# Layer 1 mixer of a decoder trunk: key rotation of all row tiles in one set of operations, and projection pieces put in other places

## The chip, the cores and the metric

The kernel runs on one core of a Trainium2 chip. The metric is the time of one execution in microseconds (us). TensorE (PE in the profile) does the matrix products, VectorE (DVE), ScalarE (ACT) and GpSimd (POOL) the element-wise work, and SyncE (SP) issues the DMA transfers. Each engine works through its own list of instructions in order; semaphores make one wait for another.

## The reference

The program is a trunk of two layers for 512 rows of width 1024. Layer 0 mixes with two kinds of attention, layer 1 with a sparse attention whose keys an indexer picks; each layer ends in an MLP and a gated embedding (PLE). The change lies in the mixer of layer 1:

```python
cq, ckv, krope, kidx, widx = split_cols(h @ w_in, C_SPLITS)   # 384, 256, 32, 64, 8
cq, ckv = rms(cq, g_cq), rms(ckv, g_ckv)
q  = (cq @ w_uq).reshape(Bn, S, 16, 96)          # 64 plain + 32 rotated
k_rope = rope(krope)                              # 32, shared by the heads
qi = partial_rope((cq @ w_qi).reshape(Bn, S, 8, 64), pos)
ki = partial_rope(kidx)                           # 64, shared
score = einsum('bqh,bqhs->bqs', wi, relu(qi . ki)) # then causal mask, top 128 of each row
# 16 heads: softmax over the picked keys, values from ckv @ w_uv, keys from ckv @ w_uk
# layer end of PLE: h += sigmoid(h @ w_ple_gate) * (p @ w_ple_proj)
```

## The kernel before

Rows are held in four tiles of 128 (`NR` = 4). Every float32 product is taken as three matmuls of split operands (high by high, high by low, low by high; `mm3`, recorded at line L213). A weight is loaded as `raw`, cast to its high part `wh` on ACT (L139), and the low part `wl` is a subtraction (L143) on DVE or, where the table says "p", on POOL in two halves of 512 columns. The class `Stream` does this in the order in which weights are listed, four tiles ahead; `FILL_ENG` holds the engine of each weight of the fill described below. Its `raw` buffers are refilled by DMAs that SP issues in order, each after the last reader of the buffer.

The mixer of layer 1 runs like this:

- `proj(xc, 360, ...)` gives ckv, key parts and index weights of each row tile. `ckv_evac` takes them out; per row tile, `k_parts(r)` rotates the key parts into `kk` with eight DVE operations (L1179 to L1187).
- `proj(cqT, 512, ...)` gives the index queries of row tiles 1 to 3. `qi_evac` rotates them (`rope32`, L557 to L562); at row tile 2 it also transposes the last ckv tile (`lat`, L254) and the keys (`kib`, `krb`, L1210 and L1211).
- `weave(indexer(), queries())` is the scheduler of this part: the indexer yields how much slack it leaves, and pieces of the fill `queries()` are put in for it. The indexer transposes the index queries (`trq`, L1233), takes the scores (`sc`), adds them up over heads into `work` (L1253 on DVE for block 1, L1256 on POOL for blocks 2 and 3), and picks the 128 largest of each row in 16 rounds of MAX8 (L1260) and MATCH_REPLACE8 (L1261) on DVE for each of the three blocks. The fill is 8 pieces of the PLE projection (`ple`), 24 of `w_uq`, 8 of `w_uv`, 8 of `w_uk` (`kn`). The rotated part of `w_uq` is rotated on DVE (L557, L558) and added on POOL (L562).
- `head_pipe` then runs 16 heads in four stages A to D (query transposes, scores and softmax, transposes of the probabilities, values), each head a step apart (`ORDER_C`). A stage step yields its slack too; the fill there is the output projection.

PE's order is the order of the code. The other engines' instructions are ordered by a scheduler of the framework, each list fixed in advance.

Of the kernel before, what the change touches and what calls it, by code (L numbers as in the profile page):

```python
# [18 lines left out]
P = 128  # L19
# [18 lines left out]
A_SLACK = 2.6  # L38
B_SLACK, B_END = 1.1, 0.7
C_END = 0.7  # L40
IDX_SLACK = (0.2, 0.8, 1.0)
ORDER_B = (("A", 3), ("B", 1), ("C", -1), ("D", -2))
ORDER_C = (("A", 3), ("B", 2), ("C", 0), ("D", -1))
# [2 lines left out]
WARM = 10  # L46


FILL_ENG = "vppvvvvpppppp"
Z_ENG = "v" * KF  # L50
SUMS = 6
G_ENG = "vvvvvvvv"
# [6 lines left out]
def trunk_kernel(ctx, tc, A, out):  # L59
# [15 lines left out]
    def bank(tag, name):  # L75
        return psum.tile([P, 512], F32, tag=tag, name=name)
# [13 lines left out]
    def f32(ap):  # L90
        return ap.bitcast(F32)
# [88 lines left out]
    for i in range(2):  # L180
        if i == 1:
            for j in range(4):
                ws.add(A["w_cq"][j], 768)
            for j in range(4):
                ws.add(A["w_ckv"][j], 720)
            ws.add(A["w_qi"][0], 1024)
            ws.add(A["w_qi2"], 512)
            fe = FILL_ENG
            add_ple(1, fe[0:3])
            for j, c in enumerate(UQ_ORDER):  # L190
                ws.add(A["w_uq"][c], 1024, fe[3 + 2 * j])
                ws.add(A["w_uq2"][c], 512, fe[4 + 2 * j])
            for c in range(2):
                ws.add(A["w_uv"][c], 1024, fe[9 + c])
            for c in range(2):
                ws.add(A["w_uk"][c], 1024, fe[11 + c])
        for j in range(8):
            ws.add(A["w_oc" if i else "w_oab"][j], 1024)
        for j in range(KF):
            ws.add(A[f"w_mi{i}"][j], 1024, Z_ENG[j])  # L200
        wo, lo, hi = A[f"w_mo{i}"], slice(0, 512), slice(512, 1024)
        for j in range(KF // 2):
            ws.add(tsum[i, j, 0], 1024)
# [236 lines left out]
    def head_pipe(small, n, order, on, stA, kk, bias, scale, vHL, oHL, ptile, ptT, slack=0.0, end=0.0, done=None, scored=None, paired=False):  # L440


        q, p, tr, o = {}, {}, {}, [None]
# [65 lines left out]
        for i in range(-3, n + 4):  # L509
            for what, d in order:  # L510
                if 0 <= i + d < n:
                    stages[what](i + d)
            yield slack if i + order[1][1] < n else end

    def ple_proj(i, stage):

# [600 lines left out]
    with ExitStack() as ctx2:  # L1117
# [8 lines left out]
        with tc.tile_pool(name="idx", bufs=1) as ip:  # L1126
# [25 lines left out]
            def latent_t(t, r, n, xt):  # L1152
                transpose_rows(xt, lambda k: t[:, k * P : (k + 1) * P], r, list(range(n // P)))
# [16 lines left out]
            kxr = kxk[:, NR * 2 * P : NR * 2 * P + NR * 96].rearrange("p (r d) -> p r d", r=NR)  # L1170
            pool.memset(kk[:, :, 1, :], 0.0)

            def k_parts(r):
                x = kxr[:, r, :].rearrange("p (h d) -> p h d", d=32)[:, 0:2, :]
                rot = ip.tile([P, 2, 32], F32, tag="rot", bufs=2, name="rot")
                m2 = ip.tile([P, 2, 32], F32, tag="m2k", bufs=2, name="m2k")
                cs = cs32[:, r, :]
                cosb = cs[:, 0:16].unsqueeze(1).to_broadcast([P, 4, 16])
                vec.tensor_tensor(rot.rearrange("p h (t d) -> p (h t) d", d=16), x.rearrange("p h (t d) -> p (h t) d", d=16), cosb, op=ALU.mult)  # L1179
                for t in range(2):  # L1180
                    sn = cs[:, (1 + t) * 16 : (2 + t) * 16].unsqueeze(1).to_broadcast([P, 2, 16])
                    vec.tensor_tensor(m2[:, :, t * 16 : (t + 1) * 16], x[:, :, (1 - t) * 16 : (2 - t) * 16], sn, op=ALU.mult)
                vec.tensor_tensor(kk[:, r, 1, 32:64], rot[:, 0, :], m2[:, 0, :], op=ALU.add)
                vec.tensor_tensor(kk[:, r, 0, 0:32], rot[:, 1, :], m2[:, 1, :], op=ALU.add)
                vec.tensor_copy(kk[:, r, 0, 32:64], kxr[:, r, 64:96])
                vec.tensor_copy(kk[:, r, 0, 64:128], kk[:, r, 0, 0:64])
                vec.tensor_copy(kk[:, r, 1, 64:96], kk[:, r, 1, 32:64])  # L1187

            def ckv_evac(r, ps):
                if r == 0:  # L1190
                    latent_t(lat[3], 3, 384, cqT)
                else:
                    latent_t(lat["kv"], r - 1, 256, ckvT)
                act.activation(kxr[:, r, :], ps[:, 256:352], AF.Copy, scale=rstd1[:, r : r + 1])
                vec.tensor_scalar(widx[:, r, :], ps[:, 352:360], rstd1[:, r : r + 1], WI_SCALE, op0=ALU.mult, op1=ALU.mult)
                lat["kv"] = latent(ps, r, 256, 1, gckv)
                k_parts(r)

            drain(proj(xc, 360, [2] * 4, range(NR), ckv_evac))

# [2 lines left out]
            qi = slot(6, "qi").rearrange("p (r d) -> p r d", d=512)  # L1203

            def qi_evac(r, ps):
                if r == 2:
                    latent_t(lat["kv"], 3, 256, ckvT)
                    kib, krb = bank("B", "kib"), bank("B", "krb")
                    for t in range(NR):
                        pe.transpose(kib[:, t * P : (t + 1) * P], kk[:, t, 0, :], ident)  # L1210
                        pe.transpose(krb[:, t * P : (t + 1) * P], kk[:, t, 1, :], ident)  # L1211
                    for h, l, b in ((kiH, kiL, kib), (krH, krL, krb)):
                        act.copy(h, b)
                        vec.tensor_tensor(l, b, f32(h), op=ALU.subtract)
                qv = qi[:, r - 1, :].rearrange("p (h d) -> p h d", d=64)
                pv = ps.rearrange("p (h d) -> p h d", d=64)
                rope32(ip, pv[:, :, 0:32], 8, cs32[:, r, :], qv[:, :, 0:32], vec)
                act.copy(qv[:, :, 32:64], pv[:, :, 32:64])


            drain(proj(cqT, 512, [2, 1], range(1, NR), qi_evac))

            work = slot(7, "work")
            knT = [slot(12 + q, f"kn{q}").rearrange("p (a s) -> p a s", s=S) for q in range(2)]
# [39 lines left out]
            def queries():  # L1264
# [16 lines left out]
                for c in range(2):  # L1281
                    u = ws.next()
                    for q in range(4):
                        ps = bank("A", "kn")
                        for k in range(2):
                            w = slice(k * 512 + q * P, k * 512 + (q + 1) * P)
                            mm3(ps, u[0][:, w], u[1][:, w], ckvT.h(k), ckvT.l(k), k == 0, k == 1)
                        yield 1.3
                        act.copy(knT[c][:, q, :], ps)
                    ws.free()  # L1290

            weave(indexer(), queries())
# [37 lines left out]
        def pt_c(h):  # L1330
            if h % 2:
# [98 lines left out]
```

## Time and profile before

| what | before |
|---|---|
| median of three runs | 1318.71 us (1317.81 to 1320.31) |
| profiled execution | 1319.21 us, span 1317.4 us |
| PE busy | 1290.8 us, 98% of the span |
| DVE busy | 959.6 us, 73% |
| ACT busy | 655.5 us, 50% |
| POOL busy | 152.2 us, 12% |

A busy PE is not yet PE at its peak; the table says how full each engine is over the whole span, not what each stage waits for. The part of the change is the stretch from about 680 to 810 us of the span.

### The profile page before, as it was taken

To read this page: it belongs to the slowest core of one execution; us is meant where nothing else is said; L and a number is where in the kernel's file an instruction comes from. 1 tells how busy PE (TensorE), PEld (TensorE's weight loads), DVE (VectorE), ACT (ScalarE), POOL (GpSimd) and SP (SyncE) were. 2 spreads that over 40 slices of the span, in tenths; PEclk is the share of its full clock that TensorE was granted. 3 is DMA by queue.
4 is the path that set the end of the run, shared out by engine and by line. 5 is a ranking of instruction groups with operands and counts; after the bars stand their busy time and mean duration, and the time that the engine had idled before them with its cause. 6 is when DMAs were issued, how large, how long until landed. Compare 5 with 4: busy or idle time off the path is not lost.

```text
span 1317.4 us, 18700 instructions
## 1 busy us (share of the span) xinstructions
PE 1290.8 (98%) x6617; PEld 1085.0 (82%) x6617; DVE 959.6 (73%) x1765; ACT 655.5 (50%) x1229; POOL 152.2 (12%) x153
## 2 busy tenths in 40 slices
PE   9999989999999999999998999999999999999998
PEld 6887878888888888887897679998988888888877
DVE  6678767377555899868568998974765667988684
ACT  4244577243223455565455777863532234556642
POOL 4202101010000000000012753310100000000000
PEclk9999989999999999999999999999999999999999
DMA  8312231459888675664243331002689897556631
GB/s 294 111 64 73 64 121 57 160 183 299 301 282 306 235 263 193 195 197 133 81 154 104 112 112 49 2 33 97 240 297 308 303 307 247 195 194 192 193 111 48
DMA packets 91535, 227.73 MB, mean 173 GB/s; under 512 B 10289, under 2 KB 11441, under 8 KB 91441
## 3 DMA queue, kind: packets, MB, share of 16 engines
q1 hardware_dynamic: 91440, 226.54, 51.5%
q8 instruction: 52, 0.85, 0.3%
q14 instruction: 43, 0.34, 0.1%
HBM read 184.55 MB, written 41.94 MB: 172 GB/s over the span
## 4 chain that ended last, share of the span: by engine, by line
PE 87%; DVE 8%; ACT 2%; issue 2%; POOL 1%; DMA 1%; SPq 0%; DVEq 0%; ACTq 0%; POOLq 0%
PE z L213 26%; PE y L213 23%; PE pj L213 23%; PE sc L213 4%; PE pv L213 3%; DVE work L1261 2%; PE trp L378 2%; DVE m L1260 2%; PE tr L254 1%; DVE wl L143 1%; PE ak L213 1%; PE ple L213 1%; PE trq L398 1%; PE pva L213 1%; DMA xraw<-in_xT_dram 1%
## 5 line engine op out<-in xcount | busy, mean ns | idle before, releaser
L143 DVE TENSOR_TENSOR wl<-raw,wh 128x1024 fp32r<-128x1024 f32 (+3 forms) x246 | 297.6, 1217 | 67.0 <-ACT wh L139 64.4
L139 ACT CAST wh<-raw 128x1024 fp32r<-128x1024 f32 (+3 forms) x254 | 261.6, 1034 | 142.0 <-PE pj L213 45.5
L897 DVE TENSOR_TENSOR b<-b 128x512 f32<-128x512 f32 x128 | 87.9, 690 | 115.9 <-DMA b<-in_w_mo_dram 107.4
L213 PE MATMUL y<-wh,ah 128*128 128x512 f32 x432 | 168.3, 390 | 0.0
L213 PE MATMUL y<-wh,al 128*128 128x512 f32 x432 | 168.1, 389 | 0.0
L213 PE MATMUL y<-wl,ah 128*128 128x512 f32 x432 | 168.1, 389 | 0.0
L213 PE MATMUL pj<-wh,big 128*128 128x512 f32 (+1 forms) x444 | 152.5, 394 | 0.0
L221 POOL TENSOR_TENSOR st<-st,mhalf 128x1 f32<-128x1 f32 (+1 forms) x41 | 30.2, 738 | 858.4 <-DVE st L325 748.6
L213 PE MATMUL z<-hz1H,wh 128*128 128x512 f32 (+1 forms) x288 | 105.6, 367 | 0.2 <-ACT hz1H L260 0.2
L213 PE MATMUL z<-hz0H,wh 128*128 128x512 f32 (+1 forms) x288 | 105.6, 367 | 0.2 <-ACT hz0H L260 0.2
L213 PE MATMUL z<-hz0L,wh 128*128 128x512 f32 (+1 forms) x288 | 105.4, 366 | 0.3 <-DVE hz0L L261 0.3
L213 PE MATMUL z<-hz1L,wh 128*128 128x512 f32 (+1 forms) x288 | 105.4, 366 | 0.3 <-DVE hz1L L261 0.3
L213 PE MATMUL z<-hz0H,wl 128*128 128x512 f32 (+1 forms) x288 | 105.5, 366 | 0.0
L213 PE MATMUL z<-hz1H,wl 128*128 128x512 f32 (+1 forms) x288 | 105.3, 366 | 0.0
L213 PEld LDWEIGHTS pj<-wh,big 128*128 128x128 f32 x444 | 84.5, 192 | 18.7 <-issue 0.7
L213 PEld LDWEIGHTS y<-wh,ah 128*128 128x128 f32 x432 | 81.1, 188 | 16.8
L213 PEld LDWEIGHTS y<-wh,al 128*128 128x128 f32 x432 | 81.1, 188 | 16.7
L213 PEld LDWEIGHTS y<-wl,ah 128*128 128x128 f32 x432 | 81.1, 188 | 16.7
L864 ACT ACTIVATE a<-t 128x512 f32<-128x512 f32 x40 | 25.3, 632 | 117.8 <-DVE t L863 117.8
L213 PEld LDWEIGHTS z<-hz0L,wh 128*128 128x128 f32 x288 | 54.3, 189 | 9.3 <-DVE hz0L L261 0.5
L213 PEld LDWEIGHTS z<-hz1L,wh 128*128 128x128 f32 x288 | 54.3, 189 | 9.3 <-DVE hz1L L261 0.5
L213 PEld LDWEIGHTS z<-hz1H,wh 128*128 128x128 f32 x288 | 54.3, 189 | 9.3 <-ACT hz1H L260 0.5
(625 smaller groups left out, 2761.0 us busy)
## 6 DMA issues: line engine op xcount, KB each, us to landing
raw<-in_w_mi_dram SPq DMA_DIRECT2D x64, 512.0 KB, 5.2
b<-in_w_mo_dram SPq DMA_DIRECT2D x128, 256.0 KB, 5.1
tsum_dram<-b SPq DMA_DIRECT2D x128, 256.0 KB, 3.5
raw<-tsum_dram SPq DMA_DIRECT2D x32, 512.0 KB, 3.2
raw<-tsum_dram SPq DMA_DIRECT2D x64, 256.0 KB, 3.0
raw<-in_w_mo_dram SPq DMA_DIRECT2D x32, 512.0 KB, 3.7
raw<-in_w_ab_dram SPq DMA_DIRECT2D x20, 512.0 KB, 4.8
raw<-in_w_mo_dram SPq DMA_DIRECT2D x32, 256.0 KB, 2.6
```

The lines of the kernel that those rows point to most:

```text
L139: act.copy(h[:, :n], raw[:, :n])
L143: (pool if e == "p" else vec).tensor_tensor(l[:, c], raw[:, c], f32(h[:, c]), op=ALU.subtract)
L213: pe.matmul(ps, a, b, start=first, stop=last, skip_group_check=True)
L221: pool.tensor_tensor(dst, src, mhalf[:, :n], op=ALU.pow)
L254: pe.transpose(ps[:, i * P : (i + 1) * P], src(k), ident)
L378: pe.transpose(ps[:, i * P : (i + 1) * P], pt[:, OFF[qt] + kt * P : OFF[qt] + (kt + 1) * P], ident)
L398: pe.transpose(ps[:, r * P : (r + 1) * P], rows(r), ident)
L864: act.activation(at[-1][:, fb % 4, :], t, AF.Square)
L897: vec.tensor_tensor(d, x, y, op=ALU.subtract)
L1260: vec.max(m8, w)
L1261: vec.match_replace(w, m8, w, MARK)
```

## The change

The key parts of all four row tiles are rotated together after the last of them, by eight operations instead of thirty-two (`k_parts()`). The transposes of ckv and keys leave `qi_evac` and come as `keys_t()` after the last index query projection and one piece of the fill; two more pieces of the fill stand between them and the query transposes. The indexer is woven with 41 more pieces, and the last four (half of `w_uk`) go into the first steps of the heads, as `RAMP_C` lists them. The low parts of four `w_uq` tiles and of the first four output projection tiles go from DVE to POOL.

```diff
+RAMP_C = (0.0, 1.3, 2.6, 1.3)
-FILL_ENG = "vppvvvvpppppp"
+FILL_ENG = "vpppppppppppp"
...
-            ws.add(A["w_oc" if i else "w_oab"][j], 1024)
+            ws.add(A["w_oc" if i else "w_oab"][j], 1024, "p" if i and j < 4 else "v")
...
-            yield slack if i + order[1][1] < n else end
+            yield ramp[i + 3] if 0 <= i + 3 < len(ramp) else slack if i + order[1][1] < n else end
...
-            def k_parts(r):
-                x = kxr[:, r, :].rearrange("p (h d) -> p h d", d=32)[:, 0:2, :]
...
+            def k_parts():
+                rot, m2 = (ip.tile([P, 2 * NR, 2, 32], F32, tag=nm, bufs=2, name="k" + nm)[:, :NR] for nm in ("r1", "r2"))
+                x = kxr[:, :, 0:64].rearrange("p r (g d) -> p r g d", d=16)
...
-                k_parts(r)
+                if r == NR - 1:
+                    k_parts()
...
             def qi_evac(r, ps):
-                if r == 2:
-                    latent_t(lat["kv"], 3, 256, ckvT)
-                    kib, krb = bank("B", "kib"), bank("B", "krb")
...
-            drain(proj(cqT, 512, [2, 1], range(1, NR), qi_evac))
+            def keys_t():
+                latent_t(lat["kv"], 3, 256, ckvT)
+                kib, krb = bank("B", "kib"), bank("B", "krb")
...
+                        if q == 3:
+                            ws.free()
+                        act.copy(knT[c][:, q, :], ps)
                         yield 1.3
-                        act.copy(knT[c][:, q, :], ps)
-                    ws.free()
...
-            weave(indexer(), queries())
+            qg = queries()
+            drain(proj(cqT, 512, [2, 1], range(1, NR), qi_evac))
+            next(qg)
+            keys_t()
+            for _ in range(2):
+                next(qg)
+            weave(indexer(), itertools.islice(qg, 5 + 24 + 8 + 4))
...
-                        scored=lambda h: k_load(h // 2 + 1) if h % 2 and h < 15 else None), itertools.islice(og, 3))
+                        scored=lambda h: k_load(h // 2 + 1) if h % 2 and h < 15 else None, ramp=RAMP_C), itertools.chain(qg, itertools.islice(og, 3)))
```

How the lists move is shown at three places. The first is PE around the key transposes (`tr` the last ckv tile, `kib` and `krb` the keys, `pj` the index query projection, `ple` a fill piece). Before:

```order
L213 MATMUL pj<-wh,cqL_6089 128x512
L254 MATMUL tr<-ident,lat 128x128 x2
L1210 MATMUL kib<-ident,kxk 128x128
L1211 MATMUL krb<-ident,kxk 128x128
L1210 MATMUL kib<-ident,kxk 128x128
L1211 MATMUL krb<-ident,kxk 128x128
L1210 MATMUL kib<-ident,kxk 128x128
L1211 MATMUL krb<-ident,kxk 128x128
L1210 MATMUL kib<-ident,kxk 128x128
L1211 MATMUL krb<-ident,kxk 128x128
L213 MATMUL pj<-wh,cqH_6088 128x512
```

Of the change, the same place:

```order
L214 MATMUL ple<-wh,wl 128x512
L255 MATMUL tr<-ident,lat 128x128 x2
L1217 MATMUL kib<-ident,kxk 128x128
L1218 MATMUL krb<-ident,kxk 128x128
L1217 MATMUL kib<-ident,kxk 128x128
L1218 MATMUL krb<-ident,kxk 128x128
L1217 MATMUL kib<-ident,kxk 128x128
L1218 MATMUL krb<-ident,kxk 128x128
L1217 MATMUL kib<-ident,kxk 128x128
L1218 MATMUL krb<-ident,kxk 128x128
L214 MATMUL ple<-wh 128x512
```

The last nine matmuls of the projection now stand ahead of the transposes, with a `ple` piece between, and `ple` pieces follow.

The second is POOL while the index scores of blocks 2 (128x384) and 3 (128x512) are added up (`work`); `wl` are halves of low parts, `big` the added rotations. Before:

```order
L143 TENSOR_TENSOR wl<-raw,wh 128x512 x2
L1256 TENSOR_TENSOR work<-rl,mA 128x384
L1256 TENSOR_TENSOR work<-rl,work 128x384 x7
L1256 TENSOR_TENSOR work<-rl,mA 128x512
L1256 TENSOR_TENSOR work<-rl,work 128x512 x6
L562 TENSOR_TENSOR big<-r_6897,r_6898 128x8x64
L143 TENSOR_TENSOR wl<-raw,wh 128x512 x3
L1256 TENSOR_TENSOR work<-rl,work 128x512
```

Of the change:

```order
L144 TENSOR_TENSOR wl<-raw,wh 128x512 x5
L1256 TENSOR_TENSOR work<-rl,mA 128x384
L1256 TENSOR_TENSOR work<-rl,work 128x384 x2
L144 TENSOR_TENSOR wl<-raw,wh 128x512 x3
L1256 TENSOR_TENSOR work<-rl,work 128x384 x4
L563 TENSOR_TENSOR big<-r_6803,r_6804 128x8x64
L1256 TENSOR_TENSOR work<-rl,work 128x384
L1256 TENSOR_TENSOR work<-rl,mA 128x512
L1256 TENSOR_TENSOR work<-rl,work 128x512 x2
L144 TENSOR_TENSOR wl<-raw,wh 128x512 x3
L1256 TENSOR_TENSOR work<-rl,work 128x512 x2
```

Three halves more stand ahead of block 2; three halves and one rotation stand between its eight additions.

The third is PE after the scores of the first head (`sc` of `qc0`), with the query transposes `trq` of head 2. Before:

```order
L213 MATMUL sc<-kc,qc0H 128x512 x2
L213 MATMUL sc<-kc,qc0L 128x512
L398 MATMUL trq<-ident,big 128x128 x4
L213 MATMUL sc<-kc,qc1H 128x128 x2
L213 MATMUL sc<-kc,qc1L 128x128
```

Of the change:

```order
L214 MATMUL sc<-kc,qc0H 128x512 x2
L214 MATMUL sc<-kc,qc0L 128x512
L214 MATMUL kn<-ckvT,wh 128x512 x2
L214 MATMUL kn<-ckvT,wl 128x512
L214 MATMUL kn<-ckvT,wh 128x512 x2
L214 MATMUL kn<-ckvT,wl 128x512
L399 MATMUL trq<-ident,big 128x128 x4
L214 MATMUL sc<-kc,qc1H 128x128 x2
```

One `kn` piece of six matmuls stands here; two more follow the scores of head 1, and one the first probabilities' transposes.

## Rows read from the trace of the kernel before

**Rows 1.** The page: busy time of the engines, and the chain that ended last.

```profile
PE 1290.8 (98%) x6617; PEld 1085.0 (82%) x6617; DVE 959.6 (73%) x1765; ACT 655.5 (50%) x1229; POOL 152.2 (12%) x153
...
PE 87%; DVE 8%; ACT 2%; issue 2%; POOL 1%; DMA 1%; SPq 0%; DVEq 0%; ACTq 0%; POOLq 0%
```

**Rows 2.** Waits of PE from 690 to 800: engine, tile, releaser, total us, times, longest.

```profile
PE trq L1233 <- DVE qi L562: 2.0, 1, 2.0
PE tr L254 <- DVE lat L1149: 1.9, 1, 1.9
PE sc L213 <- ACT qc0H L400: 1.5, 1, 1.5
PE sc L213 <- DVE qc0L L401: 1.1, 1, 1.1
```

**Rows 3.** Stretches: length, busy us of PE, PEld, DVE, ACT, POOL, granted clock, DMA share.

```profile
705.20:708.60 3.40, 3.40 (x14) 3.11 (x15) 2.41 (x9) 2.06 (x5) 0.00 (x0) 0.52 0.23 90
...
710.30:712.40 2.10, 0.10 (x2) 0.05 (x2) 2.06 (x6) 1.52 (x3) 1.72 (x2) 1.00 0.00 0
712.40:775.00 62.60, 61.16 (x283) 45.27 (x284) 60.05 (x159) 46.59 (x93) 41.01 (x34) 1.00 0.38 118
...
790.80:794.10 3.30, 3.30 (x11) 2.90 (x12) 1.71 (x7) 1.51 (x5) 0.00 (x0) 0.50 0.57 164
```

**Rows 4.** Chain that ended last, from 719 to 797: start us, us, what.

```profile
719.94 1.08 PE sc L213 x9
...
772.93 1.87 DVE wl L143
...
788.89 1.22 DVE wl L143
...
790.76 3.46 PE sc L213 x10
...
794.66 1.91 PE sc L213 x12
```

**Rows 5.** DVE in order of time: block 1 summed, and a round that stands alone.

```profile
717.44 0.48 DVE L1253 SCALAR_TENSOR_TENSOR work<-rl,widx,mA 128x256 f32<-128x256 f32 x1 [0.84 <-ACT rl L1250]
...
732.41 0.43 DVE L1260 MAX8 m<-work 128x8 f32<-128x256 f32 x1
732.87 0.09 DVE L1261 MATCH_VALUE_LOAD work<-m,work 128x8 f32 x1
732.95 0.41 DVE L1261 MATCH_REPLACE8 work<-m,work 128x256 f32<-128x256 f32 x1
733.39 0.43 DVE L1260 MAX8 m<-work 128x8 f32<-128x256 f32 x1
```

**Rows 6.** DVE groups from 716.5 to 790.2: count, busy us, mean ns, idle before.

```profile
L143 DVE TENSOR_TENSOR wl<-raw,wh 128x1024 fp32r<-128x1024 f32 (+1 forms) x7 | 8.9, 1270 | 0.0
```

**Rows 7.** POOL groups from 706 to 790, as above.

```profile
L143 POOL TENSOR_TENSOR wl<-raw,wh 128x512 fp32r<-128x512 f32 x13 | 16.8, 1322 | 11.5 <-ACT wh L139 11.5
...
L562 POOL TENSOR_TENSOR big<-r,r 128x512 f32<-128x512 f32 x4 | 5.2, 1302 | 0.2 <-DVE r L558 0.2
```

**Rows 8.** POOL in order of time: block 2, first and last additions.

```profile
722.29 1.01 POOL L1256 TENSOR_TENSOR work<-rl,mA 128x384 f32<-128x384 f32 x1 [8.92 <-ACT rl L1255]
...
731.61 2.11 POOL L1256 TENSOR_TENSOR work<-rl,work 128x384 f32<-128x384 f32 x2 [0.69 <-ACT rl L1255]
```

**Rows 9.** DVE in order of time: one key rotation without and with POOL at work.

```profile
691.19 0.21 DVE L1179 TENSOR_TENSOR rot<-kxk,cs 128x64 f32<-128x64 f32 x1
...
700.96 0.85 DVE L1179 TENSOR_TENSOR rot<-kxk,cs 128x64 f32<-128x64 f32 x1
```

**Rows 10.** PE in order of time: the first `kn` piece, and what follows the eighth.

```profile
775.85 0.62 PE L213 MATMUL kn<-ckvT,wh 128*128 128x512 f32 x2
...
786.74 1.03 PE L398 MATMUL trq<-ident,big 128*128 128x128 f32 x8
```

**Rows 11.** DMA issues from 700 to 745: count, KB, us to landing.

```profile
ple_dram<-pl SPq DMA_DIRECT2D x8, 256.0 KB, 2.1
```

More of the change, by code (lines that the diff above doesn't have):

```diff
@@ L438, in pt_pair, with head_pipe @@
                 mp.tile([P, 1280], F32R, tag="ptl", bufs=1, name=name + "L"))
-    def head_pipe(small, n, order, on, stA, kk, bias, scale, vHL, oHL, ptile, ptT, slack=0.0, end=0.0, done=None, scored=None, paired=False):
+    def head_pipe(small, n, order, on, stA, kk, bias, scale, vHL, oHL, ptile, ptT, slack=0.0, end=0.0, done=None, scored=None, paired=False, ramp=()):
         q, p, tr, o = {}, {}, {}, [None]
@@ L1171, in trunk_kernel @@
             pool.memset(kk[:, :, 1, :], 0.0)
-            def k_parts(r):
-                x = kxr[:, r, :].rearrange("p (h d) -> p h d", d=32)[:, 0:2, :]
[L1175 to L1179, printed above, removed]
-                for t in range(2):
[L1181 to L1187, printed above, removed]
@@ new lines, in k_parts @@
+            def k_parts():
+                rot, m2 = (ip.tile([P, 2 * NR, 2, 32], F32, tag=nm, bufs=2, name="k" + nm)[:, :NR] for nm in ("r1", "r2"))
+                x = kxr[:, :, 0:64].rearrange("p r (g d) -> p r g d", d=16)
+                xt = kxr[:, :, 0:64].rearrange("p r (h t d) -> p r h t d", t=2, d=16)
+                mt = m2.rearrange("p r h (t d) -> p r h t d", d=16)
+                cosb = cs32[:, :, 0:16].unsqueeze(2).to_broadcast([P, NR, 4, 16])
+                vec.tensor_tensor(rot.rearrange("p r h (t d) -> p r (h t) d", d=16), x, cosb, op=ALU.mult)
+                for t in range(2):
+                    sn = cs32[:, :, (1 + t) * 16 : (2 + t) * 16].unsqueeze(2).to_broadcast([P, NR, 2, 16])
+                    vec.tensor_tensor(mt[:, :, :, t, :], xt[:, :, :, 1 - t, :], sn, op=ALU.mult)
+                for h, (t, c) in enumerate(((1, 32), (0, 0))):
+                    vec.tensor_tensor(kk[:, :, t, c : c + 32], rot[:, :, h, :], m2[:, :, h, :], op=ALU.add)
+                vec.tensor_copy(kk[:, :, 0, 32:64], kxr[:, :, 64:96])
+                vec.tensor_copy(kk[:, :, 0, 64:128], kk[:, :, 0, 0:64])
+                vec.tensor_copy(kk[:, :, 1, 64:96], kk[:, :, 1, 32:64])
@@ L1205, in qi_evac @@
             def qi_evac(r, ps):
-                if r == 2:
-                    latent_t(lat["kv"], 3, 256, ckvT)
-                    kib, krb = bank("B", "kib"), bank("B", "krb")
[L1209 to L1214, printed above, removed]
                 qv = qi[:, r - 1, :].rearrange("p (h d) -> p h d", d=64)
@@ L1218, in qi_evac @@
                 act.copy(qv[:, :, 32:64], pv[:, :, 32:64])
-            drain(proj(cqT, 512, [2, 1], range(1, NR), qi_evac))
+            def keys_t():
+                latent_t(lat["kv"], 3, 256, ckvT)
+                kib, krb = bank("B", "kib"), bank("B", "krb")
+                for t in range(NR):
+                    pe.transpose(kib[:, t * P : (t + 1) * P], kk[:, t, 0, :], ident)
+                    pe.transpose(krb[:, t * P : (t + 1) * P], kk[:, t, 1, :], ident)
+                for h, l, b in ((kiH, kiL, kib), (krH, krL, krb)):
+                    act.copy(h, b)
+                    vec.tensor_tensor(l, b, f32(h), op=ALU.subtract)
             work = slot(7, "work")
```

## The prediction

> **What bounds the kernel now.** I read the page first: PE is busy for 98% of the span, and 87% of the chain that ended last is PE's, 8% DVE's [rows 1]. So two things can shorten the run: time in which PE stands idle or runs at the lower clock, and the stretch where the chain is DVE's. Then the waits of PE in the mixer of layer 1: 2.0 us for the last rotated index query, 1.9 us for the last ckv tile, 1.5 and 1.1 us for the first head's query [rows 2], 6.5 us in all. Then the stretches: after the waits for ckv and for the first head the granted clock is 0.52 and 0.50 for 3.4 and 3.3 us, that is 1.2 instead of 2.4 GHz, so some 1.65 us of PE's work are lost each time; after the wait of 2.0 us it stays at 1.00 [rows 3].
>
> The last view decides: the chain. Up to 721 it is PE's (index scores); from there to 790.8 it is DVE's top-128 rounds and what stands between them, and only then PE's again [rows 4]. Between 712.4 and 775 DVE is busy for 60.05 of 62.60 us [rows 3]. So PE's own waits in this stretch are not what a gain must be read from. Two clocks run: when DVE can begin with block 1 (717.44 [rows 5]) and how much besides the rounds is on its list.
>
> **The change, part by part.** The sum is made along that chain, to the first low-part product of head 0 (790.76 [rows 4]), and then along PE.
>
> A. *The lead-in.* The keys' eight operations run once instead of four times, and the last nine matmuls of the index query projection come ahead of the transposes; three `ple` pieces more (1.4 us each: six matmuls at the spacing of a `kn` piece, (786.74 - 775.85)/8 = 1.36 us [rows 10]) are put between. PE has then no reason to stand for ckv or for the query: 1.9 + 2.0 us and 1.65 us of lost clock go, 5.5 us, of which the three earlier pieces use 4.2; the pauses between kinds of matmul, which I can't split, may give some tenths more. PE would reach the first index score 1.4 to 2.0 us earlier. But what is late next is ACT. It copies each `ple` piece into one of two buffers, and a buffer is free when its store has landed, 2.1 us after issue [rows 11]. SP issues these stores in order, and between them stand loads of `raw` buffers whose last reader is now POOL: two halves of 1.32 us per tile [rows 7], where DVE took about the time of one. The third and fourth copy therefore wait, and the casts of the index queries stand behind them on ACT. I take 0.9 us of gain for the start of block 1, with 0 and 2.0 us as ends.
>
> B. *Low parts off DVE.* Seven of the eight moved subtractions stand in the stretch of the chain, 8.9 us [rows 6]; the eighth stood before it. A round alone repeats every 0.98 us for 0.43 + 0.09 + 0.41 us of work [rows 5], so a subtraction hid little in its gaps, about 0.1 us each. Gain 8.0 us (7.5 to 8.9). POOL gets them: fourteen halves, 18.5 us at 1.32 us.
>
> C. *What POOL then delays.* POOL adds up block 2's scores, eight additions from 722.29 to 733.72 [rows 8], and DVE comes to this block at about 734, when the last lone round of block 1 is done [rows 5]: just in time. Now three halves and one rotation stand between the additions: 3 x 1.32 + 1.30 = 5.3 us [rows 7]. POOL's idle time there was about 3.0 us (the stretch of 11.4 us less eight times 1.05), and it begins 0.9 to 2.0 us earlier (A), say 1.4. It would end at about 735, and DVE, which is earlier by A and by one subtraction, would come at about 733.3. MAX8 of block 2 stands next on DVE's list, and the rest of block 1's rounds behind it. I take a wait of 2.0 us for block 2 and nothing for block 3, whose three halves stood before its last addition already; ends 0 and 5.3 (all of the added POOL work shows).
>
> The batch of keys itself runs beside POOL: one rotation took 0.21 us alone and 0.85 us while POOL worked [rows 9]; three such operations are dearer by 0.64 each, but PE needs the keys only after a `ple` piece, so it costs nothing; without that cover 1.9 us. The Trainium skill has a rule for it, in "SBUF — State Buffer", section "Who interferes with whom": DVE and GpSimd share one port pair, an operation of DVE that reads two SBUF operands and one of GpSimd that reads SBUF exclude each other for a whole instruction, and one with a single SBUF input is not touched. Rows 9 fit it. By that rule the top-128 rounds stay as fast beside a fuller POOL, but the casts of the first head's keys near the end, which can take the pair, could each be held for one of POOL's halves, so C would be 4.6 instead of 2.0 us.
>
> D. *The four `kn` pieces.* 4 x 1.36 = 5.4 us of PE [rows 10] leave the stretch where the chain is DVE's, where PE had room, and come behind the first head's scores, where the chain is PE's: +5.4 us. They would only be free if PE stood idle among the first heads, and after 790.8 it doesn't. One thing can pay back: if the wait ahead of head 0 gets short enough for the clock to stay, 1.65 us (scores of head 0 3.46 us at the lower clock, of head 1 1.91 us [rows 4]). I take half, -0.8 (0 to -1.65).
>
> E. *PE itself.* With four pieces gone PE is ahead of DVE by some 5 us, but the four projection banks are held longer: the rotations of `w_uq`'s second row tile stand behind the wait of C on DVE's list. PE may be the later one at head 0; +0.8 us (0 to 2.5).
>
> Sum: -0.9 - 8.0 + 2.0 + 5.4 - 0.8 + 0.8 = -1.5 us. The profiled execution took 1319.21 us; the median of the runs is 0.5 us lower, so the sum goes from 1318.71 to **1317.2 us**. The bounds added up linearly are -9 and +7, which no likely case reaches.
>
> A measurement of this kernel tells a change from none at about 0.2%, here 2.6 us: faster is under 1316.1, slower over 1321.4.
>
> **Rivals.**
> 1. *POOL keeps up.* C is 0, the stores don't hold ACT (A 2.0), the clock stays (1.65): -2.0 - 8.0 + 5.4 - 1.65 + 0.8 = -5.4, with half of it uncertain some -4.5: 1314.2 us. For it: POOL is idle for a good part of the stretch (41.01 busy of 62.60 us [rows 3]). Against: its additions come at a pace that ACT sets, and the new halves stand among them, not behind.
> 2. *PE's time alone counts.* All four waits (6.5 us) and both stretches of low clock (3.3 us) go and no new wait comes: -9.8, 1308.9 us. For it: PE is the busiest engine. Against: the chain runs through DVE for 70 us.
> 3. *POOL becomes the bound (slower).* One mechanism: POOL's list is in order, and each half put ahead of an addition delays the top-128 behind it. It decides from the point where block 2's last addition ends after about 738. Then C is 5.3, E 2.5, D is not paid back, and A brings nothing: -8.0 + 5.3 + 5.4 + 2.5 = +5.2: 1323.9 us. For it: POOL was done with block 2 only 0.5 us before DVE needed it.
> 4. *The waits only move.* The time saved ahead of the heads and the 5.4 us behind it are equal: 1318.7 us; this is the forecast with a slightly longer wait.
>
> **How the numbers follow.** The forecast (with rival 4, from which it can't be told by a measurement) has 0.48, and its own range is 1316.1 to 1320.5. Rival 1 has 0.32, rival 2 0.05, rival 3 0.15. Faster then is rivals 1 and 2, with 0.01 of the forecast's low edge: 0.38; within 0.2%: 0.47; slower: 0.15. For 8 in 10 the range reaches down to 1312.5 (rival 1 with its margin, without rival 2) and up to 1321.5 (without most of rival 3).
>
> **What would show it.** Right, if in the new profile: PE no longer waits at the last ckv tile and the index queries, and the granted clock stays at 1.00 there (A); no subtraction `wl` stands among the rounds, which end 5 to 7 us earlier against the start of block 1 or of the span (B); DVE waits 1 to 3 us for POOL's addition ahead of block 2 (C); the four `kn` pieces stand after head 0's scores, and PE is busy throughout (D). It is wrong if DVE doesn't wait for POOL at all (then rival 1), if the last of block 2's additions comes after 738 (rival 3), if PE shows new waits over 2 us among the first heads, or if block 1 begins no earlier than before.

## The result and the profile after

| | before | after |
|---|---|---|
| median of the runs | 1318.26 us (1315.68 to 1320.31, 4 runs) | 1331.47 us (1331.22 to 1334.64, 4 runs) |
| ratio to before, 95% interval | | 1.0104 (1.0089 to 1.0118) |
| profiled execution, span | 1319.21 us, 1317.4 us | 1331.24 us, 1329.5 us |

The change makes the kernel slower by 1.0%, some 13 us; predicted were 1317.2 us and at most 1321.5. One execution of 4539 us (of the run with the engines alone, below) is left out of all ratios. The page after, PE's, DVE's and POOL's busy time and the chain that ended last:

```profile
PE 1296.2 (98%) x6617; PEld 1088.5 (82%) x6617; DVE 951.3 (72%) x1733; ACT 656.6 (49%) x1229; POOL 168.3 (13%) x167
...
PE 88%; DVE 6%; ACT 2%; issue 2%; POOL 1%; DMA 1%; SPq 0%; DVEq 0%; ACTq 0%; POOLq 0%
```

Beside [rows 1] this hardly differs, and DVE is even busy for 8 us less: shares don't show the loss. The waits of PE do. The five longest from 690 to 830 us of the span (what waits, for whom: us in total, times, longest), beside [rows 2]:

```profile
PE sc L214 <- DVE r L559: 4.8, 1, 4.8
PE sc L214 <- ACT qc0H L401: 2.5, 1, 2.5
PE sc L214 <- ACT pl L531: 2.0, 1, 2.0
PE pj L214 <- ACT rl L1250: 1.6, 2, 0.9
PE rs L494 <- DVE qc4L L402: 1.4, 1, 1.4
```

The waits for `lat` and `qi` are gone. New are 4.8 us for a rotation and 2.0 us for the copy of a `ple` piece. In both PE waits for a PSUM bank: the index scores (`sc`) and the fill pieces take the same four banks in turn (the banks of tag "A" in the kernel), and a bank can be written again only when its last contents have been read, by ACT's copy or by DVE's rotation. Each wait has a stretch of low clock behind it (stretch: length, PE busy, PEld, DVE, ACT and POOL busy, the granted clock, DMA share and GB/s):

```profile
705.20:708.60 3.40, 3.40 (x22) 2.92 (x21) 3.37 (x13) 3.01 (x6) 1.61 (x2) 1.00 0.06 23
...
718.00:722.00 4.00, 4.00 (x17) 3.39 (x18) 2.73 (x6) 2.42 (x7) 0.00 (x0) 0.50 0.47 176
...
747.00:752.30 5.30, 0.52 (x3) 0.11 (x2) 5.30 (x17) 0.00 (x0) 3.90 (x5) 0.95 0.57 198
752.30:762.00 9.70, 8.94 (x18) 5.12 (x18) 6.99 (x21) 3.17 (x6) 5.02 (x4) 0.50 0.00 0
```

The first row is the stretch that had 0.52 in [rows 3]: it is at 1.00 now. The last one is the dear one: after 4.8 us without work PE runs 9.7 us at 0.50, 1.2 instead of 2.4 GHz, so with 8.9 us busy it does 4.5 us of full-clock work. By this estimate the wait and its clock cost 9 us of PE's time together. In the same way the wait of 2.0 us, which ends at 717.8, has six us at 0.50 behind it (718 to 724).

DVE's list in order of time, around what it waits for (start, us, line and operation; the idle time before it in brackets):

```profile
718.75 0.48 DVE L1253 SCALAR_TENSOR_TENSOR work<-rl,widx,mA 128x256 f32<-128x256 f32 x1 [1.76 <-ACT rl L1250]
...
724.38 1.07 DVE L1253 SCALAR_TENSOR_TENSOR work<-rl,widx,work 128x256 f32<-128x256 f32 x2 [2.20 <-ACT rl L1250]
725.49 0.43 DVE L1260 MAX8 m<-work 128x8 f32<-128x256 f32 x1
...
740.69 0.56 DVE L1260 MAX8 m<-work 128x8 f32<-128x384 f32 x1 [2.30 <-POOL work L1256]
...
748.90 0.83 DVE L1262 TENSOR_SCALAR biast<-work 128x256 f32<-128x256 f32 x1
...
750.12 0.40 DVE L559 TENSOR_TENSOR r<-pj,cs 128x256 f32<-128x256 f32 x1
...
751.76 0.40 DVE L559 TENSOR_TENSOR r<-pj,cs 128x256 f32<-128x256 f32 x1
...
765.13 1.16 DVE L1260 MAX8 m<-work 128x8 f32<-128x512 f32 x2 [5.84 <-POOL work L1256]
...
794.40 1.49 DVE L1262 TENSOR_SCALAR biast<-work 128x512 f32<-128x512 f32 x1
```

The same places in the kernel before: block 1's first round, block 3's first round and its mask.

```profile
722.08 0.43 DVE L1260 MAX8 m<-work 128x8 f32<-128x256 f32 x1
...
753.74 1.14 DVE L1260 MAX8 m<-work 128x8 f32<-128x512 f32 x2
...
788.54 0.43 DVE L1262 TENSOR_SCALAR biast<-work 128x512 f32<-128x512 f32 x1
```

The additions of block 1 begin at 718.75 (before 717.44 [rows 5]), and its first round at 725.49, 3.4 us later than before: the last two additions wait another 2.2 us, in the stretch of half clock. Block 2 waits 2.3 us for POOL, the rotations that PE's banks wait for stand behind block 1's last round (its mask is at 748.90), and block 3 begins at 765.13, where before it began at 753.74. From there to the mask of block 3 it is 29.3 us; before it was 34.8. So some 11 us are lost ahead of block 3 and 5.5 regained in it. The chain that ended last, beside [rows 4], goes through these places (start us, us, what):

```profile
748.08 0.92 DVE work L1261 x2
...
752.31 1.62 PE sc L214 x3
...
760.76 1.48 PE sc L214 x3
...
763.82 1.29 POOL work L1256
765.13 1.14 DVE m L1260 x2
```

From block 1's last rounds it goes to PE's late scores at half clock, over POOL's last addition to block 3. PE's list at head 0 and behind it:

```profile
796.55 0.47 PE L214 MATMUL sc<-kc,qc0L 128*128 128x128 f32 x1 [1.02 <-DVE qc0L L402]
...
799.67 0.63 PE L214 MATMUL kn<-ckvT,wh 128*128 128x512 f32 x2
...
803.40 0.62 PE L214 MATMUL kn<-ckvT,wh 128*128 128x512 f32 x2
...
809.51 0.71 PE L214 MATMUL kn<-ckvT,wh 128*128 128x512 f32 x2
```

Head 0's first low-part product comes at 796.55 instead of 790.76 [rows 4], +5.8 us; the `kn` pieces add 5.5 us (1.38, 2.75 and 1.39 at these three places) and the new wait at `rs` 1.4. That is +12.7 us, 0.6 more than the span grew (+12.1).

### The profile page after: what moved, and what is told of

Its sections match the earlier page's. It is cut to its first block, busy times and chain, and to the rows that moved or that the text cites. A ratio compares the mean times of both kernels' runs of the same rounds, so it can differ in the third digit from the quotient of the medians.

```text
span 1329.5 us, 18684 instructions
## 1 busy us (share of the span) xinstructions
PE 1296.2 (98%) x6617; PEld 1088.5 (82%) x6617; DVE 951.3 (72%) x1733; ACT 656.6 (49%) x1229; POOL 168.3 (13%) x167
## 4 chain that ended last, share of the span: by engine, by line
PE 88%; DVE 6%; ACT 2%; issue 2%; POOL 1%; DMA 1%; SPq 0%; DVEq 0%; ACTq 0%; POOLq 0%
PE z L214 26%; PE pj L214 23%; PE y L214 23%; PE sc L214 4%; PE pv L214 3%; PE trp L379 2%; PE ak L214 2%; DVE work L1261 1%; PE tr L255 1%; DVE m L1260 1%; PE ple L214 1%; PE trq L399 1%; POOL wl L144 1%; DVE wl L144 1%; PE pva L214 1%
## 5 line engine op out<-in xcount | busy, mean ns | idle before, releaser
L144 DVE TENSOR_TENSOR wl<-raw,wh 128x1024 fp32r<-128x1024 f32 (+3 forms) x238 | 286.7, 1211 | 68.9 <-ACT wh L140 65.9
L214 PEld LDWEIGHTS z<-hz0H,wh 128*128 128x128 f32 x288 | 54.3, 189 | 9.1 <-ACT hz0H L261 0.5
```

The costliest lines, as they stand in the source:

```text
L144: (pool if e == "p" else vec).tensor_tensor(l[:, c], raw[:, c], f32(h[:, c]), op=ALU.subtract)
L214: pe.matmul(ps, a, b, start=first, stop=last, skip_group_check=True)
```

## The experiments

Ratios are to the kernel before, run on the same chip beside it, with their 95% interval; 0.1% is 1.3 us. The median of the kernel before differs by up to 1.2 us from one set of runs to the next (1318.1 to 1319.3), so kernels are compared by their ratios.

**Which part loses: parts undone.** First four parts were undone or relieved in the changed kernel.

The low parts of `w_uq` back on DVE:

```diff
-FILL_ENG = "vpppppppppppp"
+FILL_ENG = "vppvvvvpppppp"
```

> The four low parts of the w_uq tiles go back from POOL to DVE; the four of the output projection stay on POOL, all else as in the changed kernel (1331.5 us). Theory 'POOL's list' (the halves among the additions of blocks 2 and 3 make DVE late, and through DVE's rotations the projection banks and PE): the wait of 2.3 us at block 2 and most of PE's 4.8 us behind the rotations go, with the low clock behind it (some 4.8 us); three subtractions of 1.27 us come back among DVE's rounds: 1331.5 - 2.3 - 4.8 - 4.8 + 3.8 = about 1323.5 us, and block 3 begins some 8 us earlier. Rival 'stores' (PE is late because ACT's copy of a ple piece waits for a store behind raw loads): SP still waits, only for DVE instead of POOL, so at most 2 us come back and 3.8 go: 1331 to 1335 us. Rival 'four kn pieces behind the scores': not touched, so 1335 us.

1332.67 us, 1.0110 (1.0097 to 1.0123). The moved halves of `w_uq` among the additions are not the cause: without them PE waits even longer for a rotation (7.6 us instead of 4.8), and DVE still waits for POOL (5.9 us instead of 8.1).

```profile
PE sc L214 <- DVE r L559: 7.6, 1, 7.6
...
DVE m L1260 <- POOL work L1256: 5.9, 2, 4.5
```

In the changed kernel and here, POOL itself waits for ACT, and so for the scores, ahead of block 3's last addition (3.7 us and 1.9 us): here POOL is late for block 3 because the scores come late, and the theory of POOL's list falls for it.

The `kn` pieces ahead of the heads again:

```diff
-            weave(indexer(), itertools.islice(qg, 5 + 24 + 8 + 4))
+            weave(indexer(), qg)
...
-... ramp=RAMP_C), itertools.chain(qg, itertools.islice(og, 3)))
+... ), itertools.islice(og, 3))
```

> The four kn pieces stand ahead of the heads again (no fill in the ramp), all else as in the changed kernel (1331.5 us). Theory 'kn costs what it adds' (step D as predicted: PE had room ahead of head 0): 1331.5 - 5.4 = 1326 us. Rival 'PE has no room left': PE lost some 7 us in waits and as much at the lower clock before block 3, so that ahead of head 0 it waits only 2.5 + 1.0 us for the first query; the pieces then fill these 3.5 us and push the rest on: 1331.5 - 3.5 = 1328 us. Rival 'no part in it': 1331.5 us, if PE is the late one at head 0 anyway.

1329.09 us, 1.0082 (1.0061 to 1.0103): 0.2% back, nearer to "PE has no room left". But this interval overlaps that of the changed kernel, so the gain isn't shown.

Four stages for the `ple` pieces (a stage is the buffer that a piece is copied into and stored from):

```diff
-                yield from ple_proj(1, lambda q: ip.tile([P, 512], F32, tag="pl", bufs=2, name="pl"))
+                pls = slot(13, "pls").rearrange("p (a s) -> p a s", s=S)
+                yield from ple_proj(1, lambda q: pls[:, q % 4, :])
...
```

The lines left out take the slots of `kn` only when their halves begin; so do all later runs that use one of these slots.

> ple pieces are copied into four buffers instead of two (in a slot that is idle until the last kn pieces), all else as in the changed kernel (1331.5 us). Theory 'stores': ACT no longer waits for a store (2.96 and 0.95 us), PE reaches the index scores without its wait of 2.0 us and without the 6 us at the lower clock: the scores start 3 us earlier, and if the time from there on is set by PE and ACT it comes through whole: 1328.5 us. Rival 'POOL's list': block 2's additions get their scores earlier, but the halves of the low parts stand at the same places and wait for the same loads; DVE still waits for block 2 and PE for the rotations: 1331 us, less 1 at the most.

1326.75 us, 1.0064 (1.0050 to 1.0079): 0.40% back, 5 us, where 3 were expected. What was taken away is this, in the changed kernel (the lists of SP, ACT and PE in order of time; an SP row of several issues covers the waiting between them):

```profile
698.73 11.39 SPq L156 DMA_DIRECT2D raw<-in_w_uq_dram  x4
710.17 0.42 SPq L532 DMA_DIRECT2D ple_dram<-pl  x1
...
713.60 0.60 ACT L531 ACTIVATE pl<-ple 128x512 f32<-128x512 f32 x1 [2.96 <-DMA ple_dram<-pl]
...
717.83 0.79 PE L214 MATMUL sc<-kiT,qiH 64*128 64x256 f32 x2 [1.99 <-ACT pl L531]
```

The first store stands behind four loads of `raw`, which SP can only issue as buffers come free; ACT's third copy waits for it, and behind this copy stand the casts of the index queries. With four stages DVE begins block 3 at 762.47 instead of 765.13, still after 5.83 us of waiting, and PE still waits 4.8 us for the rotation: a loss of its own.

The rotated rows copied out of their banks by ACT:

```diff
+                qt_c = slot(13, "qtc").rearrange("p (a s) -> p a s", s=S)
...
+                            t = qt_c[:, r, :]
+                            act.copy(t, ps)
-                            rope32(ip, ps.rearrange(...), ...)
+                            rope32(ip, t.rearrange(...), ...)
...
```

> ACT copies each rotated w_uq row out of its projection bank first, and DVE rotates the copy, so that the bank is free without DVE; all else as in the changed kernel (1331.5 us). Theory 'bank held': PE's wait of 4.8 us for a rotation goes and with it the lower clock up to 762 (another 4.8 us lost), block 3's scores and its last addition come up to 9 us earlier: four copies of some 0.6 us on ACT come on top: 1323 to 1325 us. Rival 'POOL's list alone': DVE comes to block 3 when POOL has its additions done, and POOL has the same halves to do: the wait of PE goes but block 3 begins no more than 2 us earlier: 1329.5 to 1331.5 us. Rival 'kn': not touched, 1331.5 us.

1333.39 us, 1.0120 (1.0104 to 1.0135). PE's wait for rotations and DVE's waits for POOL are both gone, as the theory of the held bank has it, but the time isn't back. By operation from 715 to 800 us (count, busy, mean ns of one):

```profile
L558 DVE TENSOR_TENSOR r<-qtc,cs 128x256 f32<-128x256 f32 x8 | 7.0, 875 | 2.7 <-ACT qtc L1276 2.7
...
L559 DVE TENSOR_TENSOR r<-qtc,cs 128x256 f32<-128x256 f32 x8 | 6.3, 786 | 0.0
```

The rotations, now with two operands in SBUF, take 875 and 786 ns instead of 415 and 405 in the changed kernel: 6.7 us more on DVE's list, and PE waits 10.6 us for head 0. The edit takes the wait away and brings a price of its own, so by itself it settles nothing.

**The parts alone, and the order of the fill.** Then the rotated `w_uq` tile was put second, with nothing made dearer:

```diff
-UQ_ORDER = (2, 0, 1)
+UQ_ORDER = (0, 2, 1)
```

> The changed kernel (1331.5 us) with w_uq's column tiles in the order plain, rotated, plain (before: rotated first): the eight pieces that need DVE's rotations come eight pieces later on PE, when few scores are left. Theory 'bank held' (PE stands 4.8 us behind rotations that wait on DVE's list behind block 1's rounds and POOL's block 2, and then runs at the lower clock): the wait and the clock's 4.8 us go, block 3's scores and their last addition come 8 to 10 us earlier, no instruction becomes dearer: 1322 us; PE may then wait for rotations later, which holds only fill. Rival 'POOL's list': the halves of low parts among the additions stay, DVE still waits some 2 us for block 2 and 5 us for block 3: 1329 to 1331 us.

1326.16 us, 1.0068 (1.0048 to 1.0088): 0.36% back. PE's wait for the rotation is gone and block 3 begins at 756.32; but five of the eight row tiles are rotated only from 774 to 783, PE waits 4.1 us for ACT's copies of plain pieces, and the 1322 us expected were not reached.

The pieces ahead alone (the kernel before, with `k_parts()`, `keys_t()` and the three `next(qg)`; engines and `kn` as before):

> The kernel before (1318.5 us) with the first part alone: keys rotated in one set, three ple pieces ahead; low parts on DVE as before, kn ahead of the heads. Theory 'bank held' (the pieces ahead bring the rotated w_uq rows three pieces earlier among the scores, where DVE is not yet free): a new wait of PE of 4 to 7 us for a rotation with low clock behind it, less the waits and clock saved in the lead-in (5.5 us) and plus ACT's wait for stores: about 1322 us. Rival 'POOL's list' (the halves on POOL cause the loss): none of them here, so the lead-in's gain shows: 1314 to 1317 us.

1328.13 us, 1.0078 (1.0061 to 1.0094). So three quarters of the loss are in this part, more than expected. Its waits of PE and ACT:

```profile
PE sc L214 <- DVE r L559: 7.6, 1, 7.6
PE sc L214 <- ACT pl L531: 1.7, 1, 1.7
...
ACT pl L531 <- DMA ple_dram<-pl: 3.6, 2, 2.9
```

Both new waits are there without any of the moved low parts. The batch of keys was not run apart from the pieces.

The engines alone (the kernel before, with `FILL_ENG` and the `w_oc` entry of the change):

> The kernel before (1318.5 us) with the low parts of four w_uq and four output projection tiles on POOL, and nothing else. Step B as predicted with C of 2: 1318.5 - 8 + 2 = 1312.5 us. Theory 'PE has little room' : the rounds end 6 us earlier, but PE waits only 1.5 + 1.1 us for head 0 and loses 1.65 us of clock there, so it gains no more than that: 1314 to 1315 us. Rival 'POOL's list' (the halves among the additions make DVE and PE late): 1322 us or more.

The median is 1319.60 us, the ratio 1.0001 (0.9990 to 1.0012): nothing. Its DVE list at block 3's first round and mask, and PE's at the query transposes of head 0:

```profile
754.48 0.69 DVE L1260 MAX8 m<-work 128x8 f32<-128x512 f32 x1 [3.34 <-POOL work L1256]
...
784.89 1.54 DVE L1262 TENSOR_SCALAR biast<-work 128x512 f32<-128x512 f32 x1
```

```profile
787.24 1.03 PE L398 MATMUL trq<-ident,big 128*128 128x128 f32 x8
```

The rounds do end earlier (the mask is at 784.89 instead of 788.54), by less than half of the 8 us of step B: block 3 alone waits 3.3 us for POOL, although no rotation is late for PE by more than 1.3 us here. PE comes to the query transposes no earlier, at 787.24 instead of 786.74 [rows 10], since its waits for `lat` and `qi` (1.9 us each) are still there. Behind them it now waits 1.1 and 0.3 us for the first query, where it waited 1.5 and 1.1: 1.2 us were to be won there.

The ramp alone (the kernel before, with `RAMP_C` and four `kn` pieces behind the heads' scores):

> The kernel before (1318.5 us) with the four kn pieces behind the scores of heads 0 to 2, and nothing else. Step D as predicted: DVE's rounds set the start of head 0 either way, the pieces add 4 x 1.36 us behind: 1318.5 + 5.4 = 1324 us. Rival 'PE sets it': PE reaches head 0 late anyway and the pieces only change places: 1318 to 1319 us.

1322.41 us, 1.0036 (1.0023 to 1.0049): 3 to 6.5 us, which holds the 5.4 of step D. Its longest wait of PE shows that the pieces had filled idle time ahead of head 0:

```profile
PE sc L214 <- ACT qc0H L401: 6.9, 1, 6.9
```

The three parts alone give 0.78 + 0.01 + 0.36 = 1.15%, together 1.04%: within the noise they add up.

**Repairs.** Now four `w_uv` pieces, whose banks ACT alone empties, were put ahead of the rotated ones:

```diff
+            ws.add(A["w_uv"][0], 1024, fe[9])
             for j, c in enumerate(UQ_ORDER):
...
+                yield from values(0)
                 for c in UQ_ORDER:
...
-                for c in range(2):
-                    yield from proj(ckvT, 512, [2], range(NR), ...)
+                yield from values(1)
```

> The changed kernel (1331.5 us) with the four pieces of the first w_uv tile (ACT alone empties their banks) put between the ple and the rotated w_uq pieces: the rotated rows then reach PE one piece later than in the kernel before, not three pieces earlier; stores, engines and kn as in the changed kernel. Theory 'bank held': PE's wait of 4.8 us for a rotation shrinks to 1 us or so, the lower clock behind it goes (4.8 us), block 3 begins at 755 to 757 instead of 765: 1322 us. Rival 'POOL's list': the halves among the additions stay where they are, block 3 begins at 762 or later: 1329 to 1331 us.

1326.76 us, 1.0074 (1.0056 to 1.0093). Block 3 begins at 755.5 and the wait for a rotation is down to 1.3 us, as the theory of the held bank has it, but the 1322 us expected were not reached. ACT's wait for stores grew:

```profile
PE sc L214 <- DVE r L559: 1.3, 1, 1.3
...
ACT pl L531 <- DMA ple_dram<-pl: 7.9, 2, 4.8
```

Hence the next: values first, four stages, `kn` ahead of the heads.

> As the run before (values first), with four ple stages and with kn ahead of the heads again: all three losses taken out, the keys' batch, the pieces ahead and POOL's low parts kept. If the losses add up (bank held 9.6, stores 4.7, kn 2.4 to 3.5 us): 1331.5 - 9.6 - 4.7 - 3 = 1314 us, faster than the kernel before. Rival 'PE sets the end of the fill': PE's total work is unchanged and it can win no more than its waits in the lead-in and at head 0 (1.9 + 2.0 + 2.6 us and 3.3 us of clock) less what waits are left: not below 1312, and 1316 to 1318 if block 3's wait for POOL (3.3 us with the engines moved alone) stays.

1315.95 us, 0.9995 (0.9985 to 1.0006): the whole loss is won back, and no gain is shown. Then the low parts of `w_uq` on DVE again (`FILL_ENG` of before), and in a further run those of `w_oc` too:

> As the run before (three repairs), but the low parts of the w_uq tiles on DVE again; those of the output projection stay on POOL. 'DVE sets the end': three subtractions of 1.27 us come back among the rounds: 3.8 us later, 1318 us against 1314. 'PE sets the end' (with the engines moved alone the time did not fall though the rounds ended 3.6 us earlier): within 1 us of the run before.

> As the run before, with all low parts on DVE as in the kernel before: what is left of the change is the keys' batch, the pieces ahead, values first and four stages. 'DVE sets the end': the rounds end 8 us later than with three repairs, about where they ended before: 1318 to 1320 us. 'PE sets the end': 1314 to 1316 us.

1316.13 us, 0.9985 (0.9972 to 0.9998), and 1321.10 us, 1.0021 (1.0010 to 1.0032). The `w_uq` part brings nothing that shows; the `w_oc` part brings 0.36%, 5 us.

**What is left of the pieces ahead.** To part the held bank from the stores, the values went ahead in the run with the pieces ahead alone:

> The run with the pieces ahead alone (1328.1 us; engines and kn as in the kernel before, two stages), with the four values pieces ahead of the rotated w_uq pieces. 'Bank held, by the place of the rotated pieces alone, whatever POOL does': PE's wait of 7.6 us for a rotation goes to about 1 us and the lower clock behind it goes: 1319 to 1321 us, what is left being ACT's waits for stores. Rival 'the pieces ahead cost by something else' (ACT's waits for stores, the clock in the lead-in): 1326 us or more.

1325.68 us, 1.0044 (1.0031 to 1.0058), 5 us over what was expected. The rotation's wait went from one of 7.6 us to two of 1.7 us in all; what is left looks like the stores again. The lists of SP and ACT in order of time:

```profile
700.83 12.75 SPq L156 DMA_DIRECT2D raw<-in_w_uq_dram  x4
713.63 4.28 SPq L532 DMA_DIRECT2D ple_dram<-pl  x3
...
716.97 0.60 ACT L531 ACTIVATE pl<-ple 128x512 f32<-128x512 f32 x1 [4.99 <-DMA ple_dram<-pl]
```

Block 1 begins at 721.07. So eight stages (slots 12 and 13, each idle until its `kn` half), which no copy can wait for, in that run and in the two best:

```diff
-                yield from ple_proj(1, lambda q: ...)
+                def stage(q):
+                    if q % 4 == 0:
+                        pls.append(slot(13 - q // 4, f"pls{q}").rearrange("p (a s) -> p a s", s=S))
+                    return pls[-1][:, q % 4, :]
+                yield from ple_proj(1, stage)
```

> The run with the pieces and the values ahead (1325.7 us; engines and kn as in the kernel before), with eight stages instead of two. In that run PE's wait for a rotation had gone from 7.6 to 1.7 us, but ACT's wait for a store had grown to 5.0 us and block 1 began 4.1 us later. If the stores were what was left: block 1 begins at 716 instead of 721 and the half clock behind it goes: 1325.7 - 5 - 2 = 1318 to 1319 us, the time of the kernel before, with DVE's list (all low parts) setting the end. If it was something else: 1324 us or more.

1318.16 us, 0.9992 (0.9982 to 1.0002), as expected: no wait for stores, block 1 at 716.18, so the rest was the stores. The pieces ahead lose 0.78%; the values first give 0.34% of it back, the stages 0.52%.

> The best run so far (values first, four stages, kn ahead, w_uq low parts on DVE: 1316.1 us) with eight stages, so that no copy of a ple piece waits for a store (1.4 us on ACT and PE in that run, and some 2 us lost at the lower clock behind it). If the lead-in sets the start of block 1 and all behind it: 1316.1 - 1.4 - 1.7 = 1313 us. If DVE's or PE's own work behind it sets the end: 1315 to 1316 us.

> The run with three repairs (1316 us; all moved low parts on POOL) with eight stages. Lead-in sets the time: 1313 us. POOL sets it (DVE waited 1.9 us for block 2 there): 1315 to 1316 us, since the additions of block 2 come at POOL's pace.

1312.59 us, **0.9943** (0.9928 to 0.9958), and 1313.23 us, 0.9948 (0.9933 to 0.9964). Both are faster than both kernels, by 0.57 and 0.52% against the one before. The first of them differs from the run with 1318.16 us only in the low parts of four `w_oc` tiles, on POOL instead of DVE. The mask of block 3 on DVE's list in order of time, and then PE's wait for head 0, in the run with all low parts on DVE:

```profile
788.76 0.43 DVE L1262 TENSOR_SCALAR biast<-work 128x512 f32<-128x512 f32 x1
```

```profile
PE sc L214 <- ACT qc0H L401: 6.5, 1, 6.5
```

The same two with those of `w_oc` on POOL:

```profile
783.59 1.10 DVE L1262 TENSOR_SCALAR biast<-work 128x512 f32<-128x512 f32 x1
```

```profile
PE sc L214 <- ACT qc0H L401: 1.8, 1, 1.8
```

The rounds end 5.2 us earlier, and here the time follows (0.49%; the medians differ by 5.6 us), since PE is waiting for them for 6.5 us. In the kernel before, only 1.2 us of PE's wait was to be won. With all moved low parts the four cases stand side by side: engines alone 1.0001, lead-in repaired alone 0.9992, both 0.9948 (the second of these two runs).

## Why the prediction was wrong, by its steps

- **A failed in its price.** What it said PE would gain came true: no wait for `lat` and `qi`, and clock 1.00. It also named what is late next, ACT's copy waiting for a store behind loads of `raw`. But it took 0.9 us of gain with 0 as the worse end. The additions of block 1 began 1.3 us later, since ACT's copies had waited 2.96 and 0.95 us, and the first round came 3.4 us later, since PE's wait of 2.0 us had 6 us of half clock behind it. Two slips: the store was priced with its landing of 2.1 us alone [rows 11], where its place on SP behind four loads counted, and a new wait was not given the price that [rows 3] show for the old ones. That the loads wait for POOL's new halves was not the reason: the wait is there with the engines of before too (2.9 us).
- **E failed, and this is the larger one.** "The rotations of `w_uq`'s second row tile stand behind the wait of C" is what happened, priced at 0.8 us (0 to 2.5). It cost 4.8 us of waiting and about as much again by the clock. I looked for the harm at head 0, where PE had room; but the scores of block 3 come from PE too, so DVE's chain was late with it: block 3 began 11.4 us later, A's 3.4 among them. And the cause wasn't C: with the pieces ahead and no moved low part PE waits 7.6 us. It is the order of the fill: three pieces put ahead bring the rotated rows three pieces earlier among the scores, when DVE is still in block 1's rounds; with four other pieces in between (values first), the waits were 1.3 to 1.7 us in all. The lists are fixed in advance and could have shown this place; I counted the pieces' time, not what each needs from DVE.
- **B was right as work on DVE's list, and its 8 us did not come as time.** No `wl` stands among the rounds. But the sign named for it, rounds that end 5 to 7 us earlier against the start of block 1 or of the span, failed: they end some 4.5 and 5.9 us later. The 29.3 instead of 34.8 us behind the start of block 3 is not B alone either: three subtractions (4.4 us) have left that stretch, and so have two rounds of block 2 and four rotation instructions that now stand ahead of it. With the engines alone the rounds ended 3.65 us earlier and the time stayed. The prediction took DVE as the one bound up to head 0 and gave PE 5 us of room with four pieces moved away; PE waited only 2.6 us for head 0 [rows 2], and the low parts paid only where the lead-in was repaired too.
- **C had the number for block 2** (2.3 us against 2.0), **in good part by luck.** With the pieces ahead and no moved halves DVE still waits 1.4 us there, and with the halves moved alone it doesn't wait for block 2 at all. **For block 3 it was wrong** (5.8 us against nothing): 3.3 us come with the halves alone, 4.5 with the pieces alone. The casts of the first head's keys, which the prediction feared dearer beside POOL, took 0.40 and 0.96 us before and after; the mask grew in their place (last section).
- **D was right in size**: 5.5 us of pieces behind the scores, and alone 0.36%, 4.7 us. Its term for the clock was not: nothing was paid back, the granted clock at head 0 was 0.53 (796.55 to 799.67).
- **The range.** The ends named for the terms add up to -7.2 and +5.7, not to -9 and +7. Even the worse end gives 1324.4 us, 7 short of what was measured: A had no loss in its ends, and E no more than 2.5 us.
- **The rivals.** Rival 3 had the side right, and its point of decision was passed (block 2's last addition ended at 740.66, later than 738), but its mechanism wasn't the cause, as the run with the `w_uq` halves taken off POOL shows, and 1323.9 us was 7.6 short. Rival 2's gain is not shown: with the lead-in repaired, PE's waits for `lat` and `qi` gone and no long new one among the scores, the time stayed at 0.9992. It came only with low parts taken off DVE as well.
- **The signs named ahead** were of use: "block 1 begins no earlier than before" and a last addition of block 2 after 738 came true. "New waits over 2 us among the first heads" did not say where the harm was: the new wait of 4.8 us stands among the index scores, and at the heads the old wait for the first query grew from 1.5 to 2.5 us, and the new one at `rs` is 1.4. The prediction tied no time to the first of these signs, and gave slower as a whole 0.15, which was too little.

## What to carry to other kernels

When fill is put ahead of a critical stretch, write down for every later piece which engine empties its bank and where that engine's list stands at that time; what matters is not only how long the pieces take, but which piece now comes when. A wait of some microseconds on PE is to be priced with the half clock that this kernel's rows show behind it, which here doubled it. Where two engines' ends lie within a few microseconds, an edit on either alone can show nothing, as here (1.0001 and 0.9992), and the two together do (0.9948).

## What the runs showed of the hardware that was not expected

- The mask of block 3 (L1262, 128x512) took 1.49 us in the changed kernel, beside two halves of a low part on POOL from 794.34, and 0.43 us in the kernel before with no POOL work beside it; in the best run 1.10. It stands on the path to head 0. The Trainium skill, "SBUF — State Buffer", section "Who interferes with whom", counts `tensor_scalar` among the operations that can take the port pair shared with GpSimd; these rows agree. MAX8 and MATCH_REPLACE8 of 512 columns kept their times (means of 0.68 to 0.70 and 0.67 to 0.68 us) in all runs.
- The same rotation took 405 to 415 ns with one operand in PSUM, and 786 and 875 ns in the mean with both in SBUF. That POOL's work made the difference and not the place of the operands is shown by the sixteen instructions of that run one by one: eleven of the twelve beside POOL's work took 0.83 to 1.20 us (the other 0.42), and the four where POOL stood idle 0.40 to 0.41. One of each (POOL is idle from 764.3 to 766.4):

```profile
761.99 1.20 DVE L558 TENSOR_TENSOR r<-qtc,cs 128x256 f32<-128x256 f32 x1
...
765.08 0.41 DVE L558 TENSOR_TENSOR r<-qtc,cs 128x256 f32<-128x256 f32 x1
```

  The Trainium skill, "SBUF — State Buffer", section "Who interferes with whom", says that a DVE instruction with two SBUF inputs contends with a GpSimd instruction that reads SBUF; these rows agree.
- A store of 256 KB landed 2.1 us after issue in the kernel before [rows 11], 2.7 in the changed kernel as a median from 700 to 735 us, and 3.4 in the run with the pieces and the values ahead and two stages (705 to 722). What makes it longer no run shows.
